# Block sums of the FFN output weights by accumulating transfers, block sums of the hidden values on DVE

## The chip, the core and the metric

One of the cores of a Trainium2 chip runs the whole program; the others are idle. The time is device microseconds of one execution. Three executions of the kernel before gave 2398.52, 2399.59 and 2401.42 us, so its median is 2399.59 us.

## The reference

A decoder trunk of four layers on x of 256 tokens by 1024, all in float32. Every layer is `h += 0.5 * rmsnorm(FFN_a(rmsnorm(h)))`, then `h += rmsnorm(mixer(rmsnorm(h)))`, then a second FFN like the first. The mixers are sliding-window attention (layers 0 and 3), gated linear attention (layer 1) and RWKV-7 (layer 2). The part that matters here is the FFN, which runs eight times with weights of its own:

```
gate, up = split(x @ w_in, 2)          # x 256 x 1024, w_in 1024 x 5632
out = (silu(gate) * up) @ w_out        # w_out 2816 x 1024
```

## The kernel before, in words

**The FFN in chunks.** `ffn` (L746) cuts the 2816 hidden columns into 11 chunks of 256. For a chunk it forms the 256 hidden values of all 256 tokens from `w_in`, and multiplies them with the chunk's 256 rows of `w_out`. Every product is done in three float32r passes: each operand is split into a high part (a rounding copy on ACT) and a low part (a subtraction on DVE), and `mm3` (L606) adds high*high, high*low and low*high in PSUM.

**Seven products instead of eight.** Both factors of the second product are 2 by 2 blocks: the hidden values in blocks of 128 columns by 128 tokens, `w_out` in four blocks of 128 rows by 512 columns (256 KB each), called b11, b12, b21, b22. A Strassen-like scheme needs seven block products with seven left and seven right factors. The right ones are b11, b21, b22 and four sums: T5 = b12 - b11, T6 = b22 - T5, T4 = b21 - T6 and T7 = b22 - b12. `weights` (L779) loads the four blocks on the SP queue, forms the four sums and splits all seven. `hidden` (L796) forms four sums of 128x128 blocks of the hidden values and splits seven blocks. In the kernel before all eight sums per chunk are `tensor_tensor` instructions of POOL (`GT`, L790 and L801 to L804): in total 352 on 128x512 and 352 on 128x128.

**The main loop** (L857 to L877) runs over chunks 2 to 10, 72 chunks in the whole program. A chunk has two halves j. In each half PE does 48 matmuls of 256 columns into one PSUM bank (a half's gate and up of all tokens); DVE multiplies the gate's sums by the norm's factor (`sg`, L868), ACT copies the up half out (`up`, L869), ACT takes tanh, two DVE instructions finish the half's hidden values (L871, L872). Then PE does products of the chunk before: 12 matmuls of 512 columns in half 0, 9 in half 1. Seven of the eight PSUM banks hold the seven accumulators, so one bank serves both halves: PE can't begin the next 48 matmuls before DVE and ACT have read the bank. Besides, each chunk needs eight 128x512 blocks of `w_in` (L768), each loaded, copied on ACT and subtracted on DVE.

**What sets the order.** `Recorder` records every operation, and `schedule` (L329) orders them for the five in-order engines with prices per instruction (`price`, L276), so the program's order is a list made before compiling. All of it is issued by `emit` at L471, which is why every row of the profile has that line, and rows are told apart by tiles: `m` is a 128x512 buffer (87 of them), `hf` a 128x256 one, `ps` a PSUM bank, `ti` small ones. A load may be placed up to 24 us of PE's work ahead of its use, and so may a split. SP issues all transfers in the kernel before.

Of the kernel before, what the change touches and what calls it, by code (L numbers as in the profile page):

```python
# [15 lines left out]
AF = mybir.ActivationFunctionType  # L16
ALU = mybir.AluOpType
# [147 lines left out]
class Recorder:  # L165
# [109 lines left out]

    def price(self, op, fn, args, kw, out, acc):  # L276

        if op.eng == "sync":
            return 60.0, acc[0][1].nbytes() / 340.0
        size = lambda a: a.free_size()  # L280
        n = max(size(a) for _, a in acc) if fn == "tensor_reduce" else size(out)
        psum = any(k == "ps" for k, _ in acc)
        column = sum(isinstance(x, (View, Virtual)) for x in [kw.get("scale"), kw.get("bias")] + list(args[2:4]))
        if op.eng == "tensor":
            if fn == "transpose":
                return 109.0, 2 * n
            k = acc[1][1].partition_size() / P
            if acc[1][1].dtype == F32R:
                return (4.0 + n * 0.4453 if n >= 256 else 107.0 + n * 0.83), n * k
            if out.partition_size() <= 64 or k == 0.5:  # L290

                op.half = True
                size = max(116.0, n * 1.82) if out.partition_size() <= 64 else max(224.0, n * 1.82)
                return size * (0.5 if self.open else 1.0), 2 * n * k
            return max(224.0, n * 1.82), 4 * n * k
        if op.eng == "scalar":
            c = (51 if acc[1][0] == "ps" else 94) + 0.833 * n
            c += 93 * column + 93 * ("accum_out" in kw)
            f = args[2]
            op.table = "ln" if f == AF.Ln else None if f in (AF.Copy, AF.Identity, AF.Square, AF.Abs) else "exp"  # L300
            return c, 0.0
        if op.eng == "vector":
            if fn == "scalar_tensor_tensor" and not isinstance(args[2], float):
                column = 1
            else:
                column = int(fn == "tensor_scalar" and not isinstance(args[2], float))
            fast = fn in ("tensor_copy", "tensor_scalar") and not psum
            return 70 + 60 * column + (0.52 if fast else 1.04) * n, 0.0
        if fn == "tensor_tensor":
            return 300 + 165.0 * n if args[3] == ALU.pow else 120 + 1.1 * n, 0.0  # L310
        if fn == "tensor_copy":
            return 60 + 3.57 * n, 0.0
        if fn == "memset":
            return 36 + 0.42 * n, 0.0
        return 165 + 0.8 * n + 9 * (n / out.shape[-1]), 0.0
# [13 lines left out]
    def schedule(self):  # L329


        ops, n = self.ops, len(self.ops)
# [6 lines left out]
        for k in bufs:  # L339
            if occ[k].max() > bufs[k]:  # L340
                w = order[min(int(occ[k].argmax()), n - 1)]
# [13 lines left out]
        while len(result) < n:  # L355
            now = ops[order[front]].key
            for e in dirty:
                b, least, blocked = None, 0.0, False
                for p, i in cand[e]:
# [3 lines left out]
                    o = ops[i]  # L363
# [65 lines left out]
                half = o.half  # L429
            clock[e] = s + d  # L430
            o.start, o.end = s, s + d
            if e == "sync":
                dma = max(dma, s) + o.lat
                o.end = dma + 2000.0
            result.append(i)
# [45 lines left out]
class Trunk:  # L481
# [264 lines left out]
    def ffn(self, l, f, start):  # L746
# [10 lines left out]
        w_out = self.a["ffn_w_out"][l, f].rearrange("(k p) n -> p k n", p=P)  # L757
        n0 = 6 * l + 4 * f
        uh, ul = ([self.m2([P, 2, NT, P], F32R) for _ in range(4)] for _ in "hl")
        GT = nc.gpsimd.tensor_tensor  # L760

        def load_in(c, k):
            return self.once(("ffn", l, f, c, k), lambda: self.weight(
# [14 lines left out]

        def weights(c):  # L779

            b = {}
            nc.kind = "load"
            for j in range(2):
                for i in range(2):
                    w = b[2 - j, i + 1] = self.m2()
                    nc.sync.dma_start(w[:], w_out[:, 2 * c + j, i * 512:(i + 1) * 512])
            nc.kind = "split"
            T = {n: self.m2() for n in (1, 2, 3, 4)}
            for n, x, y in ((1, b[1, 2], b[1, 1]), (2, b[2, 2], T[1]), (4, b[2, 1], T[2]), (3, b[2, 2], b[1, 2])):
                GT(T[n][:], x[:], y[:], ALU.subtract)  # L790
            r = {n: split(w[:], lambda: self.m2(dt=F32R)) for n, w in (
                (1, b[1, 1]), (2, b[2, 1]), (3, b[2, 2]), (5, T[1]), (6, T[2]), (7, T[3]), (4, T[4]))}
            nc.kind = None
            return r

        def hidden(th):  # L796

            a12, a22, a11, a21 = (th[:, j, t, :] for j in range(2) for t in range(NT))
            S = self.m2([P, 4, P])
            s = [None] + [S[:, n, :] for n in range(4)]  # L800
            GT(s[1], a21, a22, ALU.add)  # L801
            GT(s[2], s[1], a11, ALU.subtract)
            GT(s[3], a11, a21, ALU.subtract)
            GT(s[4], a12, s[2], ALU.subtract)  # L804
            three = th[:].rearrange("p j t n -> p (j t) n")[:, :3]
            x = split(three, lambda: self.m2([P, 3, P], F32R))
            y = split(S[:], lambda: self.m2([P, 4, P], F32R))
            return {n: tuple(v[:, m, :] for v in z) for n, z, m in (
                (1, x, 2), (2, x, 0), (4, x, 1), (5, y, 0), (6, y, 1), (7, y, 2), (3, y, 3))}
# [928 lines left out]
```

## Time and profile before

| | |
|---|---|
| median of three runs | 2399.59 us |
| the profiled execution, its own time | 2397.45 us |
| its span from first to last instruction | 2395.5 us |
| mean granted TensorE clock | 0.958 |
| busy: PE, DVE, ACT, POOL | 2109.6, 2029.5, 1368.8, 899.8 us |
| DMA: bytes, share of 16 engines | 352.82 MB, 48.9% |

The profiled execution spends 2 us outside its span and stands 2.1 us under the median. Busy time of an engine is the union of its instructions; matmuls overlap in PE's pipeline, so a busy PE is not one at its peak. "Idle before" is time in which an engine had nothing running, with the instruction that ended it.

### The profile page before, as it was taken

The page shows a single profiled execution, that of the slowest core. Times are in us where ns is not written, and L with a number is a line of the kernel's source. Part 1 is how long each engine was busy: PE and PEld are TensorE (multiplying, and loading weights), DVE is VectorE, ACT ScalarE, POOL GpSimd, SP SyncE. Part 2 cuts the span into 40 slices and gives each one's busy share as a digit, 9 for nine tenths or more (in the row PEclk, how much of TensorE's full clock was granted, in tenths as well). Part 3 has the DMA queues.
Part 4 walks back from the last instruction along what each step waited for, and adds up shares of the span by engine and source line. Part 5 has one row for each costly group of instructions (what it writes and reads, how often), then busy time and mean ns, then how long its engine had stood idle before and what let it go on. Part 6 is the DMA issues. An engine that isn't in the chain of part 4 may idle for free. (4 is left out here: it accounts for less than half of the span.)

```text
span 2395.5 us, 41720 instructions
## 1 busy us (share of the span) xinstructions
PE 2109.6 (88%) x14120; PEld 1818.6 (76%) x14120; DVE 2029.5 (85%) x3292; ACT 1368.8 (57%) x3000; POOL 899.8 (38%) x889
## 2 busy tenths in 40 slices
PE   7888998888888998988888889998888888898887
PEld 6787768786777776877678768887877678777776
DVE  8887989888987988888888798588888987888887
ACT  6554666555654865555554566565555655566553
POOL 4443035435543005442644222135442544205442
PEclk8999999999999999999999999999999999999998
DMA  7555345554564454555455421454555455444551
GB/s 229 155 163 178 123 148 157 159 154 139 163 175 148 123 171 136 161 162 160 134 171 151 140 89 54 126 171 128 162 160 160 136 167 170 139 148 148 161 161 57
DMA packets 444902, 355.47 MB, mean 148 GB/s; under 512 B 33372, under 2 KB 364304, under 8 KB 444688
## 3 DMA queue, kind: packets, MB, share of 16 engines
q1 hardware_dynamic: 444688, 352.82, 48.9%
q8 instruction: 110, 1.80, 0.3%
q14 instruction: 104, 0.85, 0.1%
HBM read 351.64 MB, written 1.05 MB: 147 GB/s over the span
## 5 line engine op out<-in xcount | busy, mean ns | idle before, releaser
L471 PE MATMUL ps<-m,m 128*128 128x256 f32 (+4 forms) x12248 | 1976.2, 326 | 217.4 <-ACT hf L471 139.1
L471 PEld LDWEIGHTS ps<-m,m 128*128 128x128 f32 (+2 forms) x12248 | 1665.7, 193 | 457.8 <-ACT hf L471 177.6
L471 DVE TENSOR_TENSOR m<-m,m 128x512 fp32r<-128x512 f32 (+1 forms) x1814 | 1385.1, 816 | 148.3 <-ACT m L471 144.8
L471 ACT ACTIVATE m<-m 128x512 fp32r<-128x512 f32 (+4 forms) x1838 | 1003.8, 610 | 437.0 <-POOL m L471 335.2
L471 POOL TENSOR_TENSOR m<-m,m 128x512 f32<-128x512 f32 (+1 forms) x528 | 656.9, 1258 | 351.3 <-DMA m<-in_ffn_w_out_dram 194.6
L471 POOL TENSOR_TENSOR m<-m 128x128 f32<-128x128 f32 x176 | 131.1, 764 | 534.2 <-DVE m L471 321.1
L471 ACT ACTIVATE hf<-ps 128x256 f32<-128x256 f32 (+1 forms) x166 | 62.3, 377 | 266.4 <-DVE hf L471 244.4
L471 POOL TENSOR_TENSOR ti<-ti,nhalf 128x1 f32<-128x1 f32 (+2 forms) x60 | 50.9, 849 | 379.6 <-DVE ti L471 371.3
L471 ACT ACTIVATE m<-ps 128x512 f32<-128x512 f32 (+4 forms) x219 | 109.5, 525 | 134.2 <-PE ps L471 132.6
L471 DVE SCALAR_TENSOR_TENSOR hf<-hf,hf 128x256 f32<-128x256 f32 x144 | 99.6, 692 | 60.1 <-ACT hf L471 60.0
L471 DVE TENSOR_TENSOR m<-hf,hf 128x256 f32<-128x256 f32 x144 | 115.5, 802 | 5.0
L471 POOL TENSOR_SCALAR_AFFINE_SELECT m<-m 128x512 f32<-128x512 f32 (+1 forms) x54 | 38.6, 733 | 182.7 <-ACT m L471 182.3
L471 DVE TENSOR_TENSOR m<-m,ps 128x512 f32<-128x512 f32 (+1 forms) x112 | 60.4, 568 | 25.3 <-PE ps L471 23.3
L471 ACT ACTIVATE hf<-hf 128x256 f32<-128x256 f32 x144 | 58.9, 409 | 40.0 <-DVE hf L471 40.0
L471 DVE TENSOR_TENSOR hf<-ps,m 128x256 f32<-128x256 f32 x144 | 59.7, 415 | 21.7 <-PE ps L471 17.2
L471 PE MATMUL ps<-ident,m 128*128 128x128 f32 (+1 forms) x344 | 58.8, 281 | 4.7 <-DVE m L471 3.7
L471 ACT ACTIVATE m<-ps,gT 128x128 fp32r<-128x128 f32 (+1 forms) x192 | 53.6, 377 | 15.4 <-PE ps L471 9.1
L471 PEld LDWEIGHTS ps<-ident,m 128*128 128x128 f32 (+1 forms) x344 | 41.4, 144 | 18.5 <-DVE m L471 6.4
L471 PE MATMUL ps<-ident,hf 128*128 128x128 f32 x68 | 15.2, 308 | 45.4 <-DVE hf L471 45.4
L471 DVE SCALAR_TENSOR_TENSOR m<-ps,gT,m 128x128 fp32r<-128x128 f32 x176 | 48.5, 341 | 3.8 <-ACT m L471 3.4
L471 PEld LDWEIGHTS ps<-ident,hf 128*128 128x128 f32 x68 | 7.9, 148 | 55.1 <-DVE hf L471 38.9
L471 ACT ACTIVATE junk<-h 128x512 bf16<-128x512 f32 x48 | 30.2, 629 | 29.2 <-DVE h L471 26.7
(101 smaller groups left out, 764.1 us busy)
## 6 DMA issues: line engine op xcount, KB each, us to landing
m<-in_ffn_w_in_dram SPq DMA_DIRECT2D x1152, 128.0 KB, 2.9
m<-in_ffn_w_out_dram SPq DMA_DIRECT2D x352, 256.0 KB, 3.6
m<-in_ffn_w_in_dram SPq DMA_DIRECT2D x128, 256.0 KB, 3.8
m<-in_swa_w_qkv_dram SPq DMA_DIRECT2D x48, 256.0 KB, 2.9
m<-in_rwkv_w_rkv_dram SPq DMA_DIRECT2D x48, 256.0 KB, 3.4
m<-in_gla_w_in_dram SPq DMA_DIRECT2D x40, 256.0 KB, 3.2
m<-in_swa_w_o_dram SPq DMA_DIRECT2D x32, 256.0 KB, 2.7
m<-in_norm_g_dram SPq DMA_DIRECT2D x24, 256.0 KB, 4.8
```

What stands on the lines that cost most here:

```text
L471: getattr(getattr(self.nc, o.eng), fn)(*[fix(v) for v in args], **{k: fix(v) for k, v in kw.items()})
```

## The change

- **Weights.** The four sums of a chunk are no longer POOL instructions. ACT writes the negated minuend into the buffer of the sum (`activation` Copy with scale -1), and a transfer that POOL issues reads the other block from HBM again and adds it to what stands in the buffer. T5, T6, T4 depend on each other: negate b11, add b12; negate T5, add b22; negate T6, add b21. T7 is made in the buffer that b12 was loaded into: negate in place, add b22. SP still loads four blocks per chunk. New per chunk: four ACT instructions on 128x512 and four accumulating transfers of 256 KB. Gone: four POOL instructions on 128x512.
- **Hidden values.** The four 128x128 sums are DVE instructions instead of POOL's.
- **The planner** is told that a transfer issued by POOL holds POOL for 1200 (SP's: 60) and that its data come in the same line of transfers as SP's.

```diff
--- before.py
+++ after.py
@@ -275,8 +275,8 @@
 
     def price(self, op, fn, args, kw, out, acc):
 
-        if op.eng == "sync":
-            return 60.0, acc[0][1].nbytes() / 340.0
+        if fn == "dma_start":
+            return 60.0 if op.eng == "sync" else 1200.0, acc[0][1].nbytes() / 340.0
         size = lambda a: a.free_size()
         n = max(size(a) for _, a in acc) if fn == "tensor_reduce" else size(out)
         psum = any(k == "ps" for k, _ in acc)
@@ -429,7 +429,7 @@
                 half = o.half
             clock[e] = s + d
             o.start, o.end = s, s + d
-            if e == "sync":
+            if o.calls[0][0] == "dma_start":
                 dma = max(dma, s) + o.lat
                 o.end = dma + 2000.0
             result.append(i)
@@ -757,7 +757,6 @@
         w_out = self.a["ffn_w_out"][l, f].rearrange("(k p) n -> p k n", p=P)
         n0 = 6 * l + 4 * f
         uh, ul = ([self.m2([P, 2, NT, P], F32R) for _ in range(4)] for _ in "hl")
-        GT = nc.gpsimd.tensor_tensor
 
         def load_in(c, k):
             return self.once(("ffn", l, f, c, k), lambda: self.weight(
@@ -778,18 +777,29 @@
 
         def weights(c):
 
-            b = {}
-            nc.kind = "load"
-            for j in range(2):
-                for i in range(2):
-                    w = b[2 - j, i + 1] = self.m2()
-                    nc.sync.dma_start(w[:], w_out[:, 2 * c + j, i * 512:(i + 1) * 512])
-            nc.kind = "split"
-            T = {n: self.m2() for n in (1, 2, 3, 4)}
-            for n, x, y in ((1, b[1, 2], b[1, 1]), (2, b[2, 2], T[1]), (4, b[2, 1], T[2]), (3, b[2, 2], b[1, 2])):
-                GT(T[n][:], x[:], y[:], ALU.subtract)
+            src = lambda j, i: w_out[:, 2 * c + 2 - j, (i - 1) * 512:i * 512]
+            T = {}
+
+            def load(j, i):
+                w = self.m2()
+                nc.kind = "load"
+                nc.sync.dma_start(w[:], src(j, i))
+                nc.kind = "split"
+                return w
+
+            def less(n, x, y, new=True):
+
+                T[n] = self.m2() if new else x
+                nc.scalar.activation(T[n][:], x[:], AF.Copy, scale=-1.0)
+                nc.gpsimd.dma_start(T[n][:], src(*y), accum_op=ALU.add)
+                return T[n]
+
+            b = {1: load(1, 1), 3: load(2, 2), 2: load(2, 1)}
+            t2 = less(6, less(5, b[1], (1, 2)), (2, 2))
+            less(7, load(1, 2), (2, 2), False)
+            less(4, t2, (2, 1))
             r = {n: split(w[:], lambda: self.m2(dt=F32R)) for n, w in (
-                (1, b[1, 1]), (2, b[2, 1]), (3, b[2, 2]), (5, T[1]), (6, T[2]), (7, T[3]), (4, T[4]))}
+                *b.items(), *T.items())}
             nc.kind = None
             return r
 
@@ -798,10 +808,9 @@
             a12, a22, a11, a21 = (th[:, j, t, :] for j in range(2) for t in range(NT))
             S = self.m2([P, 4, P])
             s = [None] + [S[:, n, :] for n in range(4)]
-            GT(s[1], a21, a22, ALU.add)
-            GT(s[2], s[1], a11, ALU.subtract)
-            GT(s[3], a11, a21, ALU.subtract)
-            GT(s[4], a12, s[2], ALU.subtract)
+            for o, x, y, f in ((1, a21, a22, ALU.add), (3, a11, a21, ALU.subtract), (2, s[1], a11, ALU.subtract),
+                               (4, a12, s[2], ALU.subtract)):
+                nc.vector.tensor_tensor(s[o], x, y, f)
             three = th[:].rearrange("p j t n -> p (j t) n")[:, :3]
             x = split(three, lambda: self.m2([P, 3, P], F32R))
             y = split(S[:], lambda: self.m2([P, 4, P], F32R))
```

**POOL before**, in the middle of the first FFN (the four block sums of a chunk, then its four sums of hidden values; `m` are 128x512 buffers, and the names after "waits" are the semaphores of the engines and of SP's transfers):

```order
L471 TENSOR_TENSOR m215_340_1552<-m282_339_1550,m283_338_1548 128x512 [waits DMAHW1_49,DMAHW2_49,DVE_49,Pool_49]
L471 TENSOR_TENSOR m236_341_1554<-m233_337_1546,m282_339_1550 128x512 [waits DMAHW0_49,DVE_49]
L471 TENSOR_TENSOR m239_342_1556<-m233_337_1546,m215_340_1552 128x512 [waits DVE_49,Pool_49]
L471 TENSOR_TENSOR m260_344_1560<-m242_336_1544,m239_342_1556 128x512 [waits DMAHW7_49,PE_49,Pool_49]
L471 TENSOR_TENSOR m252_368_1686<-m28_335_1542 128x128 [waits DMAHW6_49,DMAHW5_49,DVE_49]
L471 TENSOR_TENSOR m252_368_1686<-m28_335_1542 128x128
L471 TENSOR_TENSOR m252_368_1686<-m252_368_1686,m28_335_1542 128x128 [waits Pool_49]
L471 TENSOR_TENSOR m252_368_1686<-m28_335_1542,m252_368_1686 128x128 [waits Pool_49]
```

These eight rows are gone; of the first four, only the waits for loaded blocks were waits for another engine's work.

**POOL after**, at the same place. In the first four rows T5, T7, T6 and T4 of one chunk (m242, m211, m256, m215), then those of the next:

```order
L471 DMA m242_441_2087<-in_ffn_w_out_dram 128x512 [waits DMASW0_49,DMAHW1_49,DVE_49,DMAHW2_49,PE_49,Activation_49]
L471 DMA m211_438_2079<-in_ffn_w_out_dram 128x512 [waits DMASW1_49,PE_49,Activation_49]
L471 DMA m256_456_2162<-in_ffn_w_out_dram 128x512 [waits DMASW2_49,Activation_49]
L471 DMA m215_461_2201<-in_ffn_w_out_dram 128x512 [waits DMASW3_49,PE_49,Activation_49]
L471 DMA m243_490_2327<-in_ffn_w_out_dram 128x512 [waits DMAHW0_49,DMASW4_49,DMAHW7_49,PE_49,Activation_49]
L471 DMA m258_484_2299<-in_ffn_w_out_dram 128x512 [waits DMAHW2_49,DMAHW3_49,DMAHW1_49,DMAHW4_49,DMASW5_49,Activation_49]
L471 DMA m236_503_2399<-in_ffn_w_out_dram 128x512 [waits DMASW6_49,DMAHW5_49,DVE_49,DMAHW6_49,PE_49,Activation_49]
L471 DMA m274_512_2458<-in_ffn_w_out_dram 128x512 [waits DMASW7_49,PE_49,Activation_49]
```

Eight instructions per chunk became four transfers, each behind a negation of ACT.

**ACT before**, one chunk's splits. the four rows behind a wait for POOL or on m270 split the sums m263, m255, m270 and m268:

```order
L471 ACTIVATE m20_448_2059<-m277_442_2046 128x512 [waits DMAHW1_49]
L471 ACTIVATE m28_450_2063<-m237_440_2042 128x512 [waits DMAHW7_49,Activation_49]
L471 ACTIVATE m252_453_2073<-m256_441_2044 128x512 [waits DMAHW0_49,Activation_49]
L471 ACTIVATE m236_458_2117<-m263_445_2053 128x512 [waits Pool_49]
L471 ACTIVATE m274_459_2124<-m255_447_2057 128x512 [waits Activation_49,Pool_49]
L471 ACTIVATE m276_460_2127<-m270_446_2055 128x512 [waits PE_49]
L471 ACTIVATE m257_462_2136<-m268_449_2061 128x512 [waits DMAHW2_49,Pool_49]
L471 ACTIVATE m238_464_2141<-m218_444_2050 128x512 [waits DMAHW4_49,DMAHW3_49,PE_49]
L471 ACTIVATE m211_466_2150<-m280_451_2066 128x512 [waits DMAHW6_49,DMAHW5_49,PE_49]
L471 ACTIVATE hf11_39_2160<-ps3_35_2079 128x256 [waits DVE_49]
L471 ACTIVATE hf10_40_2163<-hf9_38_2156 128x256
```

The splits stood behind POOL's four sums, of which ACT did nothing.

**ACT after**, the chunk whose transfers stand above (a split of b11 is the second row, its negation the first; DMASW is the landing of a transfer that POOL issued, DMAHW of one that SP issued):

```order
L471 ACTIVATE m242_441_2087<-m245_435_2073 128x512 [waits DMAHW7_49,Activation_49]
L471 ACTIVATE m275_443_2093<-m245_435_2073 128x512
L471 ACTIVATE m264_446_2104<-m233_436_2075 128x512 [waits DMAHW0_49]
L471 ACTIVATE m259_448_2114<-m260_437_2077 128x512 [waits DMAHW1_49,Activation_49]
L471 ACTIVATE m211_438_2079<-m211_438_2079 128x512 [waits DMAHW2_49]
L471 ACTIVATE m261_451_2129<-m265_439_2081 128x512 [waits DMAHW4_49,DMAHW3_49]
L471 ACTIVATE m244_453_2149<-m248_440_2084 128x512 [waits DMAHW6_49,DMAHW5_49]
L471 ACTIVATE m256_456_2162<-m242_441_2087 128x512 [waits DMASW0_49,PE_49]
L471 ACTIVATE m26_458_2173<-m242_441_2087 128x512 [waits DVE_49]
L471 ACTIVATE m273_460_2183<-m237_444_2097 128x512 [waits DMAHW7_49,DMAHW0_49,PE_49]
L471 ACTIVATE hf11_39_2190<-ps4_35_2100 128x256 [waits DVE_49]
L471 ACTIVATE hf10_40_2193<-hf8_38_2186 128x256
```

Three of the chunk's negations are here: m242 (T5), m211 in place (T7) and m256 (T6); the last is the first row below. The rows right behind these:

```order
L471 ACTIVATE m215_461_2201<-m256_456_2162 128x512 [waits DMASW2_49]
L471 ACTIVATE m286_462_2203<-m256_456_2162 128x512
L471 ACTIVATE m277_464_2212<-m210_434_2071 128x384 [waits DVE_49,Activation_49]
L471 ACTIVATE m254_465_2220<-m211_438_2079 128x512 [waits DMASW1_49,Activation_49]
L471 ACTIVATE m29_467_2233<-m270_463_2210 128x512 [waits DVE_49,Activation_49]
L471 ACTIVATE m278_473_2255<-m216_447_2111 128x512 [waits DMAHW2_49,DMAHW1_49]
L471 ACTIVATE m21_474_2261<-m215_461_2201 128x512 [waits DMASW3_49]
L471 ACTIVATE m212_476_2270<-m233_469_2243 128x512 [waits DMAHW4_49,DMAHW3_49]
L471 ACTIVATE m271_479_2283<-m213_470_2246 128x512 [waits DMAHW6_49,DMAHW5_49]
L471 ACTIVATE m28_485_2301<-m218_471_2249 128x512 [waits DMAHW7_49,DMAHW0_49,PE_49]
L471 ACTIVATE hf12_41_2315<-ps4_36_2207 128x256 [waits PE_49]
L471 ACTIVATE m24_489_2320<-m260_472_2252 128x512 [waits DMAHW2_49,DMAHW1_49]
```

The row after these is the negation of the next chunk's b11. So ACT's queue holds, in this order, the negation for T5 (m242), six instructions, the negation for T6 (m256, behind T5's landing), four instructions, the negation for T4 (m215, behind T6's landing), five instructions, the split of T4 (m21, behind T4's landing), five instructions, and the next chunk's first negation. Chunks 2 to 10 of the eight FFNs have 64 such passages from one chunk's split of T4 to the next chunk's first negation: in 29 that negation stands five to nine rows behind the split, in 19 one to three rows behind it, and in 16 ahead of it.

## Rows read from the trace of the kernel before

**Rows 1.** The page: busy time by engine, then the span in 40 slices.
```profile
PE 2109.6 (88%) x14120; PEld 1818.6 (76%) x14120; DVE 2029.5 (85%) x3292; ACT 1368.8 (57%) x3000; POOL 899.8 (38%) x889
...
PE   7888998888888998988888889998888888898887
```

**Rows 2.** Waits of the whole span: who waited for whom, us, times, longest.
```profile
ACT hf L471 <- DVE hf L471: 284.4, 121, 8.3
...
PE ps L471 <- ACT hf L471: 139.1, 83, 4.2
...
PE ps L471 <- DVE hf L471: 91.1, 33, 6.2
```

**Rows 3.** Timeline of one chunk: start, us, engine, count, [idle before].
```profile
121.79 8.03 PE L471 MATMUL ps<-m,m 128*128 128x256 f32 x57 [0.73 <-ACT hf L471]
121.80 5.89 POOL L471 TENSOR_TENSOR m<-m,m 128x512 f32<-128x512 f32 x4 [5.21 <-DMA m<-in_ffn_w_out_dram]
...
123.42 1.41 DVE L471 TENSOR_TENSOR m<-hf,hf 128x256 f32<-128x256 f32 x1
124.74 6.50 DVE L471 TENSOR_TENSOR m<-m,m 128x512 fp32r<-128x512 f32 x7
...
127.72 1.68 ACT L471 ACTIVATE m<-m 128x512 fp32r<-128x512 f32 x3 [0.56 <-POOL m L471]
131.17 0.41 DVE L471 TENSOR_TENSOR hf<-ps,m 128x256 f32<-128x256 f32 x1
131.61 0.38 ACT L471 ACTIVATE hf<-ps 128x256 f32<-128x256 f32 x1 [2.22 <-DVE hf L471]
...
132.05 17.96 PE L471 MATMUL ps<-m,m 128*128 128x256 f32 x117 [2.23 <-ACT hf L471]
...
135.55 1.99 SPq L471 DMA_DIRECT2D m<-in_ffn_w_out_dram  x4
...
136.97 3.70 DVE L471 TENSOR_TENSOR m<-m,m 128x512 fp32r<-128x512 f32 x6 [1.55 <-ACT m L471]
...
151.93 13.19 PEld L471 LDWEIGHTS ps<-m,m 128*128 128x128 f32 x87 [2.36 <-ACT hf L471]
```

**Rows 4.** Windows: length, busy by engine, granted clock, DMA share, GB/s.
```profile
119.00:122.00 3.00, 2.27 (x10) 1.55 (x10) 2.92 (x6) 0.98 (x4) 0.20 (x1) 1.00 0.98 307
121.00:132.00 11.00, 8.08 (x58) 7.28 (x57) 10.39 (x12) 5.98 (x13) 5.81 (x4) 1.00 0.38 109
132.00:152.00 20.00, 18.03 (x118) 16.75 (x118) 17.30 (x23) 10.77 (x22) 9.17 (x8) 0.91 0.54 159
800.00:880.00 80.00, 79.58 (x561) 64.56 (x561) 74.72 (x147) 60.77 (x118) 2.15 (x2) 1.00 0.53 157
```

**Rows 5.** Instruction groups by form, whole span: busy us, mean ns | idle before.
```profile
L471 DVE TENSOR_TENSOR m<-m,m 128x512 fp32r<-128x512 f32 x1620 | 1264.9, 834 | 137.5 <-ACT m L471 136.5
...
L471 POOL TENSOR_TENSOR m<-m,m 128x512 f32<-128x512 f32 x352 | 539.4, 1553 | 344.6 <-DMA m<-in_ffn_w_out_dram 194.6 <-DVE m L471 50.7 <-ACT m L471 38.3
...
L471 DVE TENSOR_TENSOR m<-hf,hf 128x256 f32<-128x256 f32 x144 | 115.5, 802 | 5.0
L471 DVE SCALAR_TENSOR_TENSOR hf<-hf,hf 128x256 f32<-128x256 f32 x144 | 99.6, 692 | 60.1 <-ACT hf L471 60.0
...
L471 ACT ACTIVATE m<-m 128x512 f32<-128x512 f32 x56 | 33.3, 629 | 17.1 <-DVE m L471 16.9
...
L471 DVE TENSOR_TENSOR ti<-ti,ti 128x4 f32<-128x4 f32 x48 | 7.2, 159 | 2.9 <-ACT ti L471 2.3
```

**Rows 6.** The same groups of DVE in 800 to 860 us, where POOL rests.
```profile
L471 DVE TENSOR_TENSOR m<-m,m 128x512 fp32r<-128x512 f32 x33 | 21.1, 684 | 0.0
...
L471 DVE TENSOR_TENSOR hf<-m,m 128x256 f32<-128x256 f32 x14 | 5.7, 421 | 2.5 <-ACT m L471 2.3
```

**Rows 7.** The tile view of w_out: SP's issue time, and issue to landing.
```profile
L471 SPq DMA_DIRECT2D m<-in_ffn_w_out_dram x352: 327/382/1649, 16.0 to 2341.1; - x176
...
DMA to landing us min/median/max: 2.3/3.6/5.9
```

## The prediction

> **What bounds the kernel now.** I read the page first, then the waits, one chunk's timeline, windows, and the groups by form.
>
> The page shows that no engine is full: PE is busy 88% of the span and DVE 85%, and PE stands at 8 tenths in nearly all slices, with 9 in a few that mixers fill [rows 1]. The waits say who holds PE up: 139.1 + 91.1 = 230 us of PE's idle time end with an instruction that reads the shared PSUM bank, ACT's or DVE's [rows 2]. ACT's in turn mostly waits for DVE (284.4 us in the same view).
>
> The timeline shows why DVE is late. A chunk takes from 132.05 to 151.93, 19.9 us: PE runs 17.96 us for its 117 matmuls and stands for 1.9 [rows 3]. DVE should read the bank as PE finishes with it, but reaches it at 131.17, behind seven subtractions that took 6.50 us (0.93 each) while POOL's four block sums ran from 121.80; six without POOL take 3.70 (0.62 each). A product of two 128x256 blocks took 1.41. In the stretch where POOL rests, the subtraction has a mean of 684 ns [rows 6], over the span 834 [rows 5]. So POOL's sums stop DVE, DVE is late at the bank, and PE stands. PE also pays afterwards: its granted clock is 1.00 in the 11 us before the wait of 2.23 us and 0.91 in the 20 us that begin with it [rows 4], so part of those ran at 1.2 instead of 2.4 GHz.
>
> **What a chunk could cost.** At full clock 57 matmuls (48 of 256 columns, 9 of 512) take 8.03 us [rows 3], 16,896 columns; the other half has 18,432, so 8.76. A chunk of PE alone is 16.8 us, 3.1 less than now.
>
> **The change part by part.**
>
> *POOL's sums go.* The 1620 subtractions lose 834 - 684 = 150 ns each, 243 us. The 144 products of 128x256 go from 802 to about 421 ns (the quiet row of that size), 55 us, and the 144 of the form beside them from 692 to the same, 39 us [rows 5, 6]. DVE gains some 337 us.
>
> *The hidden sums come to DVE.* 352 instructions on 128x128. The nearest rows are 159 ns for 4 columns and 421 for 256 [rows 5, 6]; between them 128 columns make 0.29 us, so 102 us. Per chunk (88 of them) DVE loses 3.8 us and gets 1.2. In 31 us of two windows it is busy 27.7 [rows 4], 17.8 per chunk of 19.9; now 15.2, still under PE's 16.8. ACT no longer waits for POOL there, at no price: DVE makes the values itself.
>
> *ACT gets four negations per chunk*, 629 ns each alone [rows 5] and 0.56 in a row of others (1.68 for three, [rows 3]). It is busy 16.75 of the 31 us, 10.8 per chunk; 13.0 with them. That fits by sum.
>
> *The transfers.* Four more blocks of 256 KB per chunk, 92 MB in all, over 12 now. DMA is busy 0.54 of a chunk, 10.7 us. At its best 307 GB/s at 0.98 share a block takes 0.85 us [rows 4]: +3.4 us, or +6.8 if adding reads the block in SBUF as well and doubles it. 14.1 to 17.5 us of 16.8: loaded, perhaps full, so no shorter landings.
>
> *The new wait.* This is the term that decides. ACT's queue is in order, and the negation for T6 waits there for the landing of T5, that for T4 for T6, the split of T4 for T4. Behind each wait stand splits of `w_in` and the copy that frees PE's bank. (On POOL, in the main loop, only the next transfers stand behind one; SP issues as many loads as before.) Call one link, from the start of a negation to the landing that the next needs, L. In the 29 close passages of the order a chunk can't be shorter than three links and the six instructions from the split to the next negation, 3L + 3.4. In the 19 loose ones it is 3L + 0.9 (the split and one or two more). In the 16 where the next chain starts first, and in the eight last chunks, no chain binds, and PE's 16.8 holds.
>
> L is the negation (0.63), two hops between queues (0.12: ACT starts 0.03 us after DVE's row ends in [rows 3], a queue's issue somewhat more) and the transfer from issue to landing, S. No transfer of POOL, and none that adds, is in this trace. The nearest row is the same block brought by SP: 2.3 us at least, 3.6 in the median, 5.9 at most [rows 7]. To the median I add 0.85 for the second read of the block (its time on the engines, as above) and 0.55 for an issue by a program of POOL instead of SP's 0.38 (between 0.38 and the 1.55 of POOL's sum, nearer to SP's, since no data pass through POOL). S = 5.0, L = 5.75. Bounds: 2.3 as if it were SP's fastest, and 5.9 + 0.85 + 0.55 = 7.3.
>
> A formula speaks for less. The Trainium skill ("DMA: Bandwidth & Descriptors", section on the anatomy of one DMA on the gpsimd path) gives about 2.0 us plus the bytes over 436 GB/s, 2.6 us for this block, as an estimate from that page. By it no chain would bind and all 72 chunks would be PE's. I keep the row: the loads of the same size here land in 3.6 us in the median, among twelve others per chunk.
>
> **The sum.** Against 19.9 us: close passages 3 x 5.75 + 3.4 = 20.65, +0.75 x 29 = +22; loose ones 18.15, -1.75 x 19 = -33; the 16 and the 8 free ones -3.1 x 24 = -74. Together -85 us from the profiled execution's 2397.5, which is 2312; that execution stands 2.1 us under the median, so **2314 us**. The mixers I leave as they are (PE is at 99% there, the 800 to 880 row of [rows 4]). Each 1 us of S moves the time by 3 x 48 = 144 us; S = 5.6 gives no change.
>
> **Rivals.**
>
> 1. *The links are short and PE becomes the bound.* Up to S = 3.7 even a close passage is at 16.8. All chunks gain 3.1: -223, 2176 us. For it: SP's fastest 2.3. Against: the DMA is fuller than before. Chance 0.20 (with S up to 4).
> 2. *The chain through ACT replaces POOL's wait, and is longer: slower.* From S = 5.6 on. At S = 6.0, L = 6.75: +3.75 x 29, +1.25 x 19, -74, +59 us: 2458. At the far bound 7.3 it would be about 2645. For it: 5.9 us landings already occur, and four more blocks come. If adding costs three passes (10.2 us a chunk), DMA alone needs 20.9, slower too. Against: in the loose first half of each FFN there is room. Chance 0.26.
> 3. *POOL and DVE still collide, the other way round.* POOL's issues are held up by DVE's instructions, one of 0.68 us each time: S + 0.68, +98 us, 2412. For it: POOL's own sum takes 1.55 us beside DVE and DVE's up to 1.4 instead of 0.42, so the two do exclude each other here. Against: an issue reads no block. The Trainium skill ("SBUF — State Buffer", the section on two separate sides) has this rule: descriptors of POOL's transfers can't be written while DVE holds the shared port, which it ties to DVE's 2-port modes; no run here shows it yet. Chance 0.08.
>
> That the change does not do what it says I leave out: the order shows POOL without a block sum.
>
> **Chances and range.** Forecast (S from 4 to 5.5): 0.41. Within 0.2% (5 us), about what a measurement of this kernel can tell from no change, lies only the point S = 5.6 with a little on either side: 0.05. Faster: the forecast and rival 1, 0.61. Slower: rivals 2 and 3, 0.34. The forecast's own range is 2202 us (S = 4.0: close passages at 17.65, the rest at 16.8) to 2386 (S = 5.5). The 80% range holds rivals 1 and 3, and rival 2 up to S = 6: **2175 to 2460 us**.
>
> **What the profile would show.** DVE's 128x512 subtraction at about 684 ns all over, its busy time near 1800 us, POOL's under 500, ACT's near 1580, transfers 445 MB. Right: a landing of POOL's transfers near 5.0 us, ACT waiting for these landings in the later chunks of an FFN, chunks of 17 us early and 20 late. Wrong: S under 4 with PE waiting for nothing (rival 1), ACT's waits for the landings over 6 us each and PE's idle time grown (rival 2), or POOL's issues long where DVE is busy (rival 3).

## The result and the profile after

Four executions of the kernel before, taken beside those of the change on one chip, have a median of 2399.06 us, four of the change 2436.05 us (2434.04 to 2441.65). The ratio is **1.0159** (95% interval 1.0138 to 1.0180): slower by 37 us, where 85 us faster was forecast. The time lies inside the range of 2175 to 2460 us, and on the side of rival 2.

The page of the kernel after: busy time, the span in 40 slices, the queue of POOL's transfers (packets, MB, share of 16 engines), and the median landings.

```profile
PE 2123.7 (87%) x14078; PEld 1842.4 (76%) x14078; DVE 1750.6 (72%) x3644; ACT 1547.6 (64%) x3352; POOL 423.0 (17%) x537
...
PE   8888998888878999888988789998988888898887
...
q0 software_dynamic: 50688, 92.30, 23.2%
...
m<-in_ffn_w_in_dram SPq DMA_DIRECT2D x1152, 128.0 KB, 4.7
m<-in_ffn_w_out_dram SPq DMA_DIRECT2D x352, 256.0 KB, 5.1
m<-in_ffn_w_out_dram POOLq DMA_DIRECT2D x352, 256.0 KB, 5.2
```

DVE's share fell from 85% to 72% and POOL's work halved, as meant, and yet PE has the same 8 tenths as in [rows 1]. SP's own loads of `w_out` now land in 5.1 us in the median, 3.6 in [rows 7].

The groups of the kernel after by form: busy us, mean ns | idle before, and what ended it.

```profile
L471 ACT ACTIVATE m<-m 128x512 fp32r<-128x512 f32 x1620 | 921.4, 621 | 287.0 <-DMA m<-in_ffn_w_out_dram 252.1 <-DVE m L471 30.2 <-DMA m<-in_ffn_w_in_dram 3.2
L471 ACT ACTIVATE m<-m 128x512 f32<-128x512 f32 x408 | 250.8, 626 | 266.9 <-DMA m<-in_ffn_w_out_dram 247.4 <-DVE m L471 13.6 <-PE ps L471 5.5
L471 DVE TENSOR_TENSOR m<-m,m 128x512 fp32r<-128x512 f32 x1620 | 1030.7, 689 | 302.1 <-ACT m L471 298.7
L471 DVE TENSOR_TENSOR m<-hf,hf 128x256 f32<-128x256 f32 x144 | 61.2, 425 | 4.9
L471 DVE SCALAR_TENSOR_TENSOR hf<-hf,hf 128x256 f32<-128x256 f32 x144 | 60.9, 423 | 113.9 <-ACT hf L471 113.9
L471 DVE TENSOR_TENSOR m<-m,m 128x128 f32<-128x128 f32 x176 | 50.3, 286 | 0.0
```

The first two rows are ACT's splits and its negations (352 of the 408; the other 56 are those of [rows 5]). Both stand idle some 250 us for a landing of `w_out`. The DVE rows are what the prediction asked for: 689 ns instead of 834, 425 and 423 instead of 802 and 692 [rows 5], and a hidden sum takes 286.

The waits of the kernel after, whole span: us, times, longest.

```profile
POOL m L471 <- ACT m L471: 1050.2, 240, 39.7
ACT m L471 <- DMA m<-in_ffn_w_out_dram: 499.4, 232, 5.8
DVE m L471 <- ACT m L471: 376.3, 255, 5.1
...
PE ps L471 <- ACT hf L471: 142.6, 51, 7.9
PE ps L471 <- DVE hf L471: 111.0, 43, 4.6
...
ACT hf L471 <- DVE hf L471: 57.7, 52, 7.7
```

The second of these rows in the kernel before:

```profile
ACT m L471 <- DMA m<-in_ffn_w_out_dram: 8.7, 5, 2.4
```

The chain of who waits for whom has turned round. In [rows 2] PE waited for DVE and ACT, and ACT for DVE (284.4, now 57.7). Now DVE waits for ACT, and ACT for a landing: 499.4 us, 8.7 before. PE's wait for the readers of its bank is 142.6 + 111.0 = 254 us, somewhat more than the 230 it replaced. (POOL's waits for other engines are not all new: its block sums waited 50.7 us for DVE and 38.3 for ACT, beside 194.6 for loads [rows 5].)

One chunk in the timeline of the kernel after: start, us, engine, count, [idle before, and what ended it].

```profile
96.90 0.63 ACT L471 ACTIVATE m<-m 128x512 f32<-128x512 f32 x1 [4.96 <-DMA m<-in_ffn_w_out_dram]
...
97.82 0.87 POOL L471 DMA_DIRECT2D m<-in_ffn_w_out_dram  x1 [7.62 <-DMA m<-in_ffn_w_in_dram]
...
98.31 19.25 PE L471 MATMUL ps<-m,m 128*128 128x256 f32 x117 [3.49 <-DVE hf L471]
...
103.55 4.80 ACT L471 ACTIVATE m<-m 128x512 fp32r<-128x512 f32 x9 [2.76 <-DMA m<-in_ffn_w_out_dram]
...
104.99 0.85 POOL L471 DMA_DIRECT2D m<-in_ffn_w_out_dram  x1 [6.31 <-ACT m L471]
...
109.82 1.56 ACT L471 ACTIVATE m<-m 128x512 f32<-128x512 f32 x3 [0.74 <-DMA m<-in_ffn_w_out_dram]
...
110.75 0.85 POOL L471 DMA_DIRECT2D m<-in_ffn_w_out_dram  x1 [2.80 <-ACT m L471]
...
118.67 2.71 ACT L471 ACTIVATE m<-m 128x512 f32<-128x512 f32 x5 [4.40 <-DMA m<-in_ffn_w_out_dram]
119.59 0.87 POOL L471 DMA_DIRECT2D m<-in_ffn_w_out_dram  x1 [7.99 <-ACT m L471]
...
121.29 0.36 ACT L471 ACTIVATE hf<-ps 128x256 f32<-128x256 f32 x1
...
121.68 0.42 DVE L471 TENSOR_TENSOR hf<-ps,m 128x256 f32<-128x256 f32 x1
...
122.16 18.20 PE L471 MATMUL ps<-m,m 128*128 128x256 f32 x112 [4.60 <-DVE hf L471]
...
123.59 3.75 ACT L471 ACTIVATE m<-m 128x512 fp32r<-128x512 f32 x7 [1.04 <-DMA m<-in_ffn_w_out_dram]
```

All the links of one chain can be read here. At 96.90 ACT negates for a chunk's T4; it ends at 97.53, POOL issues at 97.82 (a hop of 0.29 us), and at 103.55 ACT, idle for 2.76, splits T4 as it lands: a link of 6.65. The second instruction of the group at 103.55, at 104.08, is the next chunk's first negation. POOL issues T5 at 104.99; T6's negation waits for it until 109.82, T4's for T6 until 118.67 (8.85 us), the split for T4 until 123.59. Behind the negation at 118.67 stands the copy that empties PE's bank, at 121.29: PE stands for 4.60. This chunk takes from 98.31 to 122.16, 23.85 us, where one took 19.9 in [rows 3].

Windows of the kernel after: length, busy by engine (PE, PEld, DVE, ACT, POOL), granted clock, DMA share, GB/s.

```profile
98.31:122.16 23.85, 19.12 (x118) 17.50 (x118) 15.11 (x30) 14.69 (x31) 3.82 (x5) 0.86 0.76 180
380.00:540.00 160.00, 132.90 (x853) 123.29 (x854) 101.75 (x205) 98.24 (x196) 28.54 (x33) 0.90 0.83 201
```

In this chunk neither DVE (15.11 of 23.85) nor ACT (14.69) is full. The granted clock is 0.86 here and was 0.91 in the chunk of [rows 4]; PE is busy 19.12 of 23.85 us here and was busy 18.03 of 20.00 there.

### The profile page after: what moved, and what is told of

Same layout as the page of the kernel before. It is cut to its first block, busy times and chain, and to the rows that moved or that the text cites. A ratio compares the mean times of both kernels' runs of the same rounds, so it can differ in the third digit from the quotient of the medians.

```text
span 2432.3 us, 42295 instructions
## 1 busy us (share of the span) xinstructions
PE 2123.7 (87%) x14078; PEld 1842.4 (76%) x14078; DVE 1750.6 (72%) x3644; ACT 1547.6 (64%) x3352; POOL 423.0 (17%) x537
## 3 DMA queue, kind: packets, MB, share of 16 engines
q0 software_dynamic: 50688, 92.30, 23.2%
## 4 chain that ended last, share of the span: by engine, by line
PE 33%; issue 33%; DMA 13%; DVE 9%; ACT 6%; POOL 5%; SPq 1%; POOLq 0%; DVEq 0%; ACTq 0%
PE ps L471 33%; DMA m<-in_ffn_w_out_dram 10%; DVE m L471 7%; ACT m L471 5%; POOL m L471 4%; DMA m<-in_ffn_w_in_dram 3%; POOL ti L471 1%; SPq L471 1%; ACT junk L471 1%; DVE hf L471 1%; ACT hf L471 1%; DVE h L471 0%; DVE ti L471 0%; POOLq L471 0%; DMA m<-in_swa_b_qkv_dram 0%
## 5 line engine op out<-in xcount | busy, mean ns | idle before, releaser
L471 PE MATMUL ps<-m,m 128*128 128x256 f32 (+4 forms) x12248 | 1997.9, 329 | 251.7 <-ACT hf L471 137.0
L471 PEld LDWEIGHTS ps<-m,m 128*128 128x128 f32 (+2 forms) x12248 | 1694.9, 196 | 484.1 <-ACT hf L471 162.3
L471 ACT ACTIVATE m<-m 128x512 fp32r<-128x512 f32 (+4 forms) x2190 | 1189.3, 611 | 568.8 <-DMA m<-in_ffn_w_out_dram 499.4
L471 DVE TENSOR_TENSOR m<-m,m 128x512 fp32r<-128x512 f32 (+3 forms) x1990 | 1176.8, 643 | 364.5 <-ACT m L471 360.1
L471 POOL DMA_DIRECT2D m<-in_ffn_w_out_dram x352 | 305.0, 888 | 1287.4 <-ACT m L471 877.5
L471 DVE SCALAR_TENSOR_TENSOR hf<-hf,hf 128x256 f32<-128x256 f32 x144 | 60.9, 423 | 113.9 <-ACT hf L471 113.9
L471 DVE TENSOR_TENSOR m<-hf,hf 128x256 f32<-128x256 f32 x144 | 61.2, 425 | 4.9
L471 DVE TENSOR_TENSOR m<-m 128x128 f32<-128x128 f32 (+2 forms) x201 | 56.7, 322 | 5.8 <-ACT m L471 3.2
L471 ACT ACTIVATE junk<-m 128x512 bf16<-128x512 f32 x40 | 24.9, 624 | 26.8 <-DVE m L471 26.8
L471 DVE SCALAR_TENSOR_TENSOR h<-m,ti,h 128x512 f32<-128x512 f32 x48 | 34.0, 746 | 5.7 <-POOL ti L471 5.5
```

Of the source, the lines that this page charges most:

```text
L471: getattr(getattr(self.nc, o.eng), fn)(*[fix(v) for v in args], **{k: fix(v) for k, v in kw.items()})
```

## The experiments

**The theory** (A in the expectations): ACT's in-order queue waits for the landings of the chained sums, because the program's order puts the next link behind too few other rows; the order was made for a landing 2.8 us after the transfer takes its turn (0.77 for the bytes and 2.0), and it takes 5.2. **Rivals:** the load of the added transfers itself (23.2% of 16 engines) makes everything late, whatever the order (B in the expectations); POOL's issues are held up by DVE; or it is the move of the hidden sums to DVE that costs.

### Which part costs: the two halves alone

First the hidden sums on DVE, with POOL still forming the block sums:

```diff
-            GT(s[1], a21, a22, ALU.add)
...
+            for o, x, y, f in ((1, a21, a22, ALU.add), (3, a11, a21, ALU.subtract), (2, s[1], a11, ALU.subtract),
+                               (4, a12, s[2], ALU.subtract)):
+                nc.vector.tensor_tensor(s[o], x, y, f)
```

> One part of the change alone: the hidden sums on DVE, the block sums as before on POOL, no adding transfer. POOL loses 249 us of small sums, DVE gets 102 us and is no longer stopped by them. Both theories: the large part of the collisions is with the block sums (539 us of POOL), so the time falls a little, to between 2370 and 2400 us.

Measured 2350.30 us, ratio 0.9812 (0.9797 to 0.9826): 44 us faster, more than expected (run e1). DVE's subtraction stays at 847 ns, so its collision is due to POOL's 128x512 sums, which are still there; in the next run, which leaves POOL only the hidden sums, it takes 699. Now the transfers, with the hidden sums left on POOL:

```diff
...
-                nc.vector.tensor_tensor(s[o], x, y, f)
...
+            nc.gpsimd.tensor_tensor(s[1], a21, a22, ALU.add)
...
```

> The other part alone: the block sums by adding transfers, the hidden sums as before on POOL. Theory A: the chain through ACT is all there, and POOL's small sums (0.7 us each) now also stand between the transfers in POOL's queue, so 2436 us or more, up to 2500. If it is faster than 2436 by over 20 us, the four sums on DVE were part of the loss.

Measured 2475.29 us, ratio 1.0339 (1.0314 to 1.0364), as expected (e2). Alone, the halves give -44 and +81, and the sum, +37, is the whole change. The transfers are the loss; ACT waits 436.8 us for them here too.

### The order: one number of the planner

```diff
-                o.end = dma + 2000.0
+                o.end = dma + (2000.0 if e == "sync" else 4500.0)
```

This says to the planner that POOL's transfers land 5.3 us after their turn. Nothing else differs: the same instructions and the same bytes, in another order.

> The changed kernel, with one number of the planner altered: the landing of a transfer that POOL issues is planned at the 5.2 us that the trace shows (median) instead of 2.8, so that the order leaves more of ACT's work between a transfer and what waits for it. Work, transfers and bytes are the same. Theory A (the chain of three transfers per chunk, waited for in ACT's in-order queue, costs the time): ACT's waits for these transfers fall from 499 us to under 250, and the time from 2436 to about 2330 or less. Theory B (the 92 MB more that the 16 engines move cost it, by late loads): the waits move elsewhere and the time stays within 2400 to 2460.

Measured **2150.81 us**, ratio 0.8974 (0.8953 to 0.8994), run e3. This is a far larger gain than I expected. Its waits (us, times, longest):

```profile
DVE m L471 <- ACT m L471: 171.0, 189, 5.8
ACT m L471 <- DMA m<-in_ffn_w_out_dram: 153.8, 110, 5.5
...
PE ps L471 <- ACT hf L471: 31.5, 24, 3.8
```

A window of its main loop (columns as in the windows above):

```profile
380.00:540.00 160.00, 156.23 (x1022) 139.39 (x1021) 137.08 (x279) 118.35 (x252) 41.84 (x67) 1.00 0.93 237
```

ACT waits 153.8 us instead of 499.4, PE 31.5 instead of 142.6 for ACT's copy, and the clock of the window is 1.00 instead of 0.90. The order explains it: of the 64 passages, 63 now have the next chunk's first negation ahead of the split of T4 (16 before), and from a negation to the next use of its sum on ACT it is 12 rows in the median, not 7 (chunks 2 to 10). The transfers are no faster, 5.8 us against 5.2, and the engines are busier, 0.93 against 0.83. So the load alone is no bound, and that rival falls.

### The chain: links without dependence

```diff
-            t2 = less(6, less(5, b[1], (1, 2)), (2, 2))
+            less(5, b[1], (1, 2))
+            less(6, b[1], (2, 2))
             less(7, load(1, 2), (2, 2), False)
-            less(4, t2, (2, 1))
+            less(4, b[3], (2, 1))
```

> The changed kernel, with T6 negated from b11 and T4 from b22 instead of from T5 and T6, so that no transfer waits for another; it leaves out the dependence, and T6 and T4 have other values. Four negations and four transfers per chunk as before. Theory A: under 2340 us, ACT's waits for these transfers under 200 us. Theory B: 2400 to 2440, since the same bytes move.

Measured 2265.18 us, ratio 0.9443 (0.9429 to 0.9457), run e4. The time is what the theory asked for, its size of ACT's wait is not: 276.8 us, where under 200 was expected. The tile view of its transfers by POOL (issue min/median/max, then issue to landing) shows why:

```profile
L471 POOL DMA_DIRECT2D m<-in_ffn_w_out_dram x352: 844/1149/1958, 24.8 to 2219.2; - x176
...
DMA to landing us min/median/max: 3.7/7.2/11.5
```

Four transfers that do not depend on each other follow one another: 236 of the 352 issues begin within 0.3 us of the end of the one before, 33 in the kernel after. The median issue then takes 1.15 us and the landing 7.2 (862 ns and 5.2 in the kernel after). A split placed for 2.8 us still waits. What goes is the waiting of the negations: by form, 30.4 us of ACT's wait stand ahead of its 128x512 f32 rows, 247.4 before.

### The floor, and the price of adding

Without the adding transfers, with the negations kept:

```diff
-                nc.gpsimd.dma_start(T[n][:], src(*y), accum_op=ALU.add)
```

> The changed kernel without the adding transfers: ACT's four negations per chunk stay, POOL issues nothing, and the sums are left out. It is the bound of what freeing DVE from POOL is worth when neither chain nor bytes are there. Both theories: DVE's 128x512 subtraction at 685 ns, PE's waits for the shared bank under 60 us, about 2180 us (72 chunks at 16.8 instead of 19.9). If it stays above 2300, something that neither theory names holds the chunk.

The busy times on its page:

```profile
PE 2019.4 (97%) x14128; PEld 1771.6 (85%) x14128; DVE 1738.2 (83%) x3644; ACT 1538.0 (74%) x3352; POOL 114.5 (5%) x185
```

Measured 2085.92 us, ratio 0.8693 (0.8679 to 0.8707), run e7: lower than I thought, with PE busy 97%. So the transfers and the waits for them cost 350 us of the kernel after, and e3 gives back 285 of them. Next, the same program with transfers that only copy; the order of every engine is that of the kernel after:

```diff
-                nc.gpsimd.dma_start(T[n][:], src(*y), accum_op=ALU.add)
+                nc.gpsimd.dma_start(T[n][:], src(*y))
```

> The changed kernel in exactly its own order on every engine, with POOL's 352 transfers copying instead of adding (the sums are left out: the block overwrites the negation). It measures what the adding itself costs in S, and what S is worth at this order. If adding reads each block a second time, a transfer of 2 KB rows takes half the engine time, its share of the engines falls from 23.2% to about 12%, and the median landing from 5.2 to some 4.3 us. Theory A at 144 us per us of S: about 2300 us. If the landing stays above 5 us, the adding is not what makes it long, and the time stays near 2436.

Measured 2233.85 us, ratio 0.9316 (0.9282 to 0.9349), run e8. The tile view of the plain transfers (issue min/median/max, then issue to landing):

```profile
L471 POOL DMA_DIRECT2D m<-in_ffn_w_out_dram x352: 536/538/724, 24.7 to 2200.5; - x176
...
DMA to landing us min/median/max: 2.7/3.9/7.7
```

The same view of the kernel after:

```profile
L471 POOL DMA_DIRECT2D m<-in_ffn_w_out_dram x352: 844/862/1369, 24.9 to 2400.6; - x176
...
DMA to landing us min/median/max: 3.6/5.2/9.2
```

The queue of the plain ones on their page (packets, MB, share of 16 engines), beside 50688 and 23.2% above:

```profile
q0 software_dynamic: 28160, 92.30, 12.9%
```

To add costs 0.32 us of issue, twice the engines' time (0.232 x 2432 / 352 = 1.60 us of all 16 per block against 0.129 x 2231 / 352 = 0.82) and 1.3 us of landing. At an unchanged order the run is 202 us faster: 155 per us of S, if all of it is put down to these 1.3 us; the prediction had 144. (SP's loads of `w_in` land sooner too, after 4.1 us instead of 4.7 in the median, but ACT waits for them only 3.2 us in the kernel after.)

### How far to plan ahead

Two more values of the planner's number, 3250 and 7000, that is 4.0 and 7.8 us after the turn:

```diff
-                o.end = dma + 2000.0
+                o.end = dma + (2000.0 if e == "sync" else 3250.0)
```

> The changed kernel with POOL's landing planned at 4.0 us, between the 2.8 of the change and the 5.2 of e3_true_landing. In its order the 64 passages between chunks are no longer 29 close, 19 loose and 16 in which the next chain starts first, but 0, 13 and 51, and a link has 10 rows of ACT in the median instead of 7. Theory A, now with the order's distance as what decides: 2200 to 2260 us with S unchanged at 5.2 to 5.8. If it is at 2151 already, any overlap of the chains is enough; if above 2350, only the last step to the true landing helps.

Measured 2230.57 us, ratio 0.9292 (0.9254 to 0.9330), in the middle as expected (e9).

> The same with 7.8 us, above the median and near the slowest tenth of the landings (7.3 us). All 64 passages have the next chain start first, a link has 15 rows in the median. Theory A: the waits for late landings shrink further, 2120 to 2150 us, unless the longer lead takes buffers from the loads. Worse than 2170 would show that price.

Measured 2264.18 us, ratio 0.9434 (0.9407 to 0.9461), run e10: worse than 5.3, against my expectation. ACT's splits and negations of this run by form (columns as above):

```profile
L471 ACT ACTIVATE m<-m 128x512 fp32r<-128x512 f32 x1620 | 915.1, 622 | 274.6 <-DMA m<-in_ffn_w_out_dram 255.9 <-DVE m L471 10.4 <-DMA m<-in_ffn_w_in_dram 6.5
L471 ACT ACTIVATE m<-m 128x512 f32<-128x512 f32 x408 | 247.3, 623 | 21.3 <-DMA m<-in_ffn_w_out_dram 11.6 <-DVE m L471 9.6
```

The negations hardly wait any more (11.6 us, 68.3 with 5.3), but the splits do (255.9, 85.5 with 5.3). Paired with their transfers, nearly all of that, 252 us, stands ahead of the split of T4: it lies in the median 6 rows behind its negation (11 with 5.3), while T6's negation lies 15 rows behind T5's and T4's 17 behind T6's. The planner gave its room to the first two links, and the last has half of what it had. The landings are longer as well, 6.4 us in the median (5.8 with 5.3). Three planned links of 7.8 us and their negations come to more than the 24 us by which a split may be ahead; that this limit is the reason I argue from the code, and no run shows it.

### Fewer links

All eight sums on DVE, in the kernel before:

```diff
-                GT(T[n][:], x[:], y[:], ALU.subtract)
+                nc.vector.tensor_tensor(T[n][:], x[:], y[:], ALU.subtract)
```

with the hidden sums as in the first experiment.

> The kernel before, with all eight sums of a chunk on DVE: no work of POOL in the chunk, no adding transfer, no negation. 352 sums of 128x512 at 0.69 us and 352 of 128x128 at 0.29 come to DVE, 345 us, against 337 us that it no longer loses to POOL. By DVE's sum per chunk 17.8 - 3.8 + 1.2 + 2.8 = 18.0 us, DVE becomes the bound: about 2290 us if DVE is kept full, 2330 to 2400 if it also waits. Theory A and B both allow this; it shows what the transfers buy over the plainest way round POOL.

> e5_all_dve once more, beside e6_half_long on one chip, to say which of the two ways round POOL is faster: 2113 us again.

Measured 2112.71 us, ratio 0.8807 (0.8794 to 0.8820), and on another chip 2112.81, ratio 0.8812 (0.8791 to 0.8833), run e5: far better than expected. DVE's 128x512 forms in the first of them (busy us, mean ns | idle before):

```profile
L471 DVE TENSOR_TENSOR m<-m,m 128x512 fp32r<-128x512 f32 x1620 | 1020.9, 685 | 22.1 <-ACT m L471 15.5
L471 DVE TENSOR_TENSOR m<-m,m 128x512 f32<-128x512 f32 x430 | 284.2, 685 | 1.8 <-ACT m L471 1.2
```

DVE does the block sums too, at 685 ns each (POOL needed 1553, [rows 5]), and is still less busy in all, 1937.4 us, than the 2029.5 of [rows 1], when POOL did them. My estimate of 18 us of DVE per chunk was wrong: from 380 to 540 us DVE is busy 153.62 of 160 and a chunk takes 16.2 in the median, 15.6 us of DVE.

Then two of the four sums by transfers, T5 and T7, which depend on no other, and T6 = b22 - T5 and T4 = b21 - T6 on DVE (`minus` makes a buffer and subtracts with `tensor_tensor`), with the landing planned at 5.3 us and at 7.8:

```diff
-            t2 = less(6, less(5, b[1], (1, 2)), (2, 2))
...
+            t1 = less(5, b[1], (1, 2))
             less(7, load(1, 2), (2, 2), False)
-            less(4, t2, (2, 1))
+            minus(4, b[2], minus(6, b[3], t1))
```

> A mix that could beat all: T5 and T7, which wait for nothing but loads, by adding transfers with their landing planned at 5.2 us; T6 and T4 as subtractions on DVE. 176 transfers instead of 352, no chain, two negations per chunk instead of four, and DVE gets 176 sums (120 us) instead of 352 (240 us). DVE's sum per chunk is about 16.4 us, ACT's 12. Theory A: nothing waits in a chain, so PE is the bound: between 2086 (no transfers at all) and 2113 us (all sums on DVE). Theory B: the 46 MB more still cost something, above 2113.

> e6_half_true (T5 and T7 by transfers, T6 and T4 on DVE) with the landing planned at 7.8 us instead of 5.2. ACT's remaining waits for these transfers (about 84 us) go; 2090 to 2104 us. The floor without any sum is 2086.

Measured 2104.39 us, ratio 0.8789 (0.8767 to 0.8811), and **2080.13 us**, ratio 0.8673 (0.8652 to 0.8695), runs e6. The second is the fastest of the kernels that leave nothing out, 32.7 us under the version with all sums on DVE on the same chip. The busy times on its page:

```profile
PE 2013.2 (97%) x14136; PEld 1762.2 (85%) x14136; DVE 1842.8 (89%) x3820; ACT 1459.4 (70%) x3176; POOL 274.4 (13%) x361
```

With one link in place of three, planning for 7.8 us helps where it hurt the chain of three. Its ratio is level with that of the run without transfers, 0.8693 (0.8679 to 0.8707). That run has two negations more per chunk and no sums on DVE, so it is not a strict floor, but little can be left of the transfers' cost.

## Why the prediction was wrong

**Right: what DVE gets back.** The subtraction was to be 684 ns and is 689, the two 128x256 forms 421 and are 425 and 423, a hidden sum 0.29 us and is 0.286. POOL is under 500 us (423.0), ACT near 1580 (1547.6). DVE's 1750.6 is 50 under the 1800. What the Trainium skill ("SBUF — State Buffer", the section on two separate sides) says of such a collision, that a DVE instruction with two inputs in SBUF contends with a POOL instruction that reads SBUF, agrees with 834 falling to 689 as POOL's sums go.

**Right: the mechanism and the price of 1 us.** ACT's in-order queue waits at T6's and T4's negations and at the split, as written. S was to be 5.0 us and has a median of 5.2, and e8 gives 155 us per us of it against 144. The adding of a block does take double the engines' time, 1.60 us against the 1.7 assumed. That is rival 2's mechanism, at nearly the forecast's own S.

**Wrong: the link L.** The prediction made L 5.75 = 0.63 + 0.12 + 5.0. Paired up in the trace, a link of T5, T6 and T4 is 0.63 for the negation, 0.34 for the hop from ACT to POOL (never under 0.29, the one in the timeline) and 5.37 for S (means; 4.96 for T5, 5.57 for the two behind it): 6.33. The hop was set from ACT behind DVE and was nearly three times that; S was taken from a median, where the mean counts. This 6.33 is all but the break-even which the prediction itself had named, S = 5.6, with its shorter hop L = 6.35: a close passage is then 22.45 us and a loose one 19.95, and +74, +1 and -74 make no change. So L alone takes away the forecast's gain, but does not make the kernel slower.

**Wrong: the 24 chunks that were to be free.** Sixteen passages with the next negation ahead and the eight last chunks were put at PE's 16.8 us, -74 in all, as if a chunk were as long as the passage from one chain to the next allows. From one chain's first negation to the next one's the trace has 21.8 us in the close passages, 20.5 in the loose ones and 15.8 in the sixteen (means), much as the sum with the measured L has it. But the chunks in which these passages lie, from DVE's first reading of the bank to its first in the next chunk, take 20.1, 22.5 and 21.6 us, where the prediction had 20.65, 18.15 and 16.8. Of the eight last chunks, the half between their two readings takes 10.0 us. So the passage does not set the length of the chunk, and a chain that starts early does not free its chunk: ACT waits for landings of `w_out` 6.1 us per chunk in the sixteen, 6.5 in the close and 8.5 in the loose ones.

The step fails because it looked only at the passage from one chain to the next: inside a chain, the next use stands a median of 7 rows behind a negation, some 4 us of ACT's work, and a link of 6.3 makes ACT wait wherever the chain stands. e3 confirms it: with 12 rows the wait falls to a third, and a chunk takes 17.4 us in the mean instead of 21.2. The sign that the prediction had named, chunks of 17 us early and 20 late, is not there: the first two of an FFN's chunks, read in this way, take 22.1 and 20.8 us.

In the sum, from DVE's first reading of the bank to its last, the main loops of the eight FFNs take 1331 us before and 1436 after, +105 instead of -85. Against the prediction's own lengths, the sixteen chunks are 76 us over, the nineteen loose ones 83 over and the 29 close ones 17 under; the rest is the eight last chunks, and that a chunk of the kernel before has a mean of 19.6 us there (1331 over 8 x 8.5), not 19.9.

**Missing: the rest of the program.** Outside the main loops the change gains 1065 - 997 = 68 us, of which the prediction had nothing: in the first FFN DVE first reads chunk 2's bank at 52.61 us of the span, before at 61.70. +105 - 68 = 37, the result. That 2436 us lies inside the stated range is no merit of the sum: the range was made wide enough for rival 2 up to S = 6, and the slowdown came at an S of 5.2.

**Rival 1** (PE alone) did not happen, and its time was too long: 2176 us, where the run without transfers takes 2086 and a chunk 16.3 us in the median, not 16.8. **Rival 3** (issues held up by DVE) is not seen. An issue takes 844 to 1369 ns, median 862. Leave aside the 33 that follow another directly, among them the longest: 17 of the others ran while DVE stood and 296 beside its `tensor_tensor`, and the median is 862 ns in both. The Trainium skill's rule of that section would have held the issues only for DVE's 2-port modes, in which DVE takes the port that it shares with POOL; `tensor_tensor`, which does most of DVE's work here, has none by the same section, and the trace agrees. The formula of the Trainium skill ("DMA: Bandwidth & Descriptors", anatomy of one DMA) gave an estimate of 2.6 us; the fastest landing here is 3.6 us adding and 2.7 plain, the medians 5.2 and 3.9, so the row was the better guide.

**What bounded the change, then,** was less the transfers or their load than an order that was made for 2.8 us. The prediction read the diff's planner lines and priced the waits that they leave as if only the passage between two chains mattered, and did not ask what the same change would be worth with a true number there: 249 us faster than before instead of 37 slower.

## What to carry to other kernels

When work is moved from an engine to a transfer, the distance in the in-order queue between the instruction that starts it and the one that needs it can decide more than any engine's share, as it did here: count the rows between them, multiply by the time of a row, and compare with the hop plus the time from issue to landing. A planner's constant for that latency belongs to the change and is to be measured under load; here 2.8, 4.0, 5.3 and 7.8 us gave 2436, 2231, 2151 and 2264 us. And ask first whether an engine that another disturbs could do the work itself: once POOL's sums were gone, DVE did them all in less total time than it had needed without them.

## What the runs showed of the hardware beyond what I expected

- A transfer of 256 KB from POOL that adds to SBUF costs 862 ns of POOL to issue, 1.60 us of all 16 engines and 144 packets (50688 / 352); the plain one 538 ns, 0.82 us and 80 packets.
- Issues of POOL that follow one another get slower: one that begins within 0.3 us of the end of another takes 1.22 us in the median in e4 (236 issues) and 1.19 in the kernel after (33), any other 0.86. With many of them, the median landing is 7.2 us instead of 5.2, at nearly the same share of the engines (24.5% against 23.2%).
- The hop from ACT's last result to POOL's issue is 0.29 us at least, ten times the 0.03 from DVE to ACT that [rows 3] shows.
- A shorter idle time of PE paid twice here: with PE busy 87% of the span in the kernel after, 88% before, 95% in e3 and 97% in the fastest version, the mean granted clock is 0.944, 0.958, 0.984 and 0.994.
